# S5 output matrix made on GpSimd, with its power chain and the S5 steps set later, in a two-block transformer kernel

## Chip, cores and metric

One core of a Trainium2 chip runs the whole program. The metric is the device time of one execution in microseconds; the kernel before takes 1207.07 us (median of 3 runs, 1204.92 to 1209.34).

## What is computed

The input is 256 tokens of width 1024. A first block mixes two branches, an S5 layer (a diagonal complex state-space scan over 32 groups of 64 states) and an mLSTM, then does cross attention and a convolutional feed-forward; two more layers follow. The change touches only the S5 branch of the first block:

```python
a_bar = jnp.exp(lam * dt)
b_bar = ((a_bar - 1.0) / lam)[..., None] * b_mat
bu = jnp.einsum('blgh,gph->blgp', ug, b_bar)
_, states = lax.associative_scan(combine, (a_seq, bu), axis=1)
y = jnp.einsum('blgp,ghp->blgh', states, c_mat).real + d * ug
```

and, beside it, the projection `proj = h @ w_in` from which the S5 input, the mLSTM's queries, keys, values and gates and the branch gates come.

## The kernel before

All matrix products are done in split float32: each weight tile is loaded to `raw` on SP's queue, ScalarE rounds it to a high half `hi` (L321), VectorE takes the low half `lo` = raw - hi (L322), and TensorE runs three matmuls per 128-row step (L329 to L331 feature-major, L338 to L340 token-major). So every weight tile of 128x1024 costs ScalarE, VectorE and TensorE one turn each. PSUM has three tiles of tag `g` for projections and four of tag `a` for small work.

The first block's projections come in this order: two pairs of tiles for the S5 input U (L1679 evacuates); four pairs for queries and keys, each evacuated by `ev_qk`: a product into `msg` (L1689), ScalarE's first tap (L1695), six taps on VectorE (L1697), ScalarE's tanh back into `msg` (L1699) and a last product (L1700). `msg` has one buffer, so the next pair's L1689 waits until the pair before is through L1700. Then the token-major columns: `w_vif` (values and mLSTM gates, 264 wide), `w_tm` 1, 2 and 3 (values, two halves of the output gate). Then come the S5 scan, the mLSTM, eight pairs of gate projections, and the S5 output.

The S5 steps lie between. `s5_prep` makes on VectorE the powers `pz` of the transition and the input factors `cz`, and on GpSimd the chain of squarings `ak`, `ax` (L719 to L723) that the scan multiplies with. `s5_inputs(b)`, for b = 0 and 1, forms from `pz`, `cz` and the constants four outer products on VectorE, each of two products and one sum or difference (L754, L755): the output matrices CR and CN, 128x640 elements each, and the input matrices, two of 128x512. ScalarE copies each into block-diagonal tiles (L764 into CR, L767 into CN, L772 into `w4`), half of the partitions at a time. TensorE then transposes (L779) and forms the short-range kernel (L785, L787), and ScalarE copies these out (L780, L790). `s5_state` passes U through DRAM into U2 by five DMAs issued on ScalarE's queue and multiplies it (L805) into the states ST. `s5_scan` combines ST in ten steps on VectorE (L815 to L818), and `s5_output` reads CR, CN, KS and ST (L842) after the gate projections.

The order of work on each engine is not written by hand. A planner gives every instruction the priority of its place in the program (raised for weight loads), goes through the program with its own estimate of durations, and puts on each engine the instruction of highest priority among those that are ready; the order is then fixed, and each engine works through its list, waiting where it must. A tile with a tag and one buffer can be given out again only when all readers of the tile before it in that tag are done. So ST, `so` (two buffers), `hs` (one) and `msg` (one) set waits as well as the data does.

Of the kernel before, what the change touches and what calls it, by code (L numbers as in the profile page):

```python
# [20 lines left out]
P = 128  # L21
# [236 lines left out]
def _program(ctx, tc, nc, a, offs, dump):  # L258
# [21 lines left out]
    mult, add, sub = ALU.mult, ALU.add, ALU.subtract  # L280
# [359 lines left out]
    def s5_prep(bp):  # L640
# [42 lines left out]
        G.memset(pz[:, 0, :, 0:1], 1.0)  # L683
        G.memset(pz[:, 1, :, 0:1], 0.0)

        def cmul(o, x_, y_, conj=False, tt=tt):
            sh = list(o.shape)
            n_ = len(sh) > 3 and sh[3] or 1
            u, v = [T(bp, sh, "cm%d_%d" % (n_, q_), bufs=2 if n_ == 1 else 1) for q_ in range(2)]
            tt(u, x_, y_, op=mult)  # L690
            tt(v, x_, y_[:, ::-1], op=mult)
            if conj:
                tt(o[:, 0], u[:, 0], u[:, 1], op=add)
                tt(o[:, 1], v[:, 1], v[:, 0], op=sub)
            else:
                tt(o[:, 0], u[:, 0], u[:, 1], op=sub)
                tt(o[:, 1], v[:, 0], v[:, 1], op=add)
# [15 lines left out]
        cmul(cz[:, :, :, 2], cz[:, :, :, 3], p1)  # L713
        cmul(cz[:, :, :, 0:2], cz[:, :, :, 2:4], sq2)
        cmul(pz[:, :, :, 3:5], pz[:, :, :, 1:3], sq2)
        NL = 5
        ak = T(bp, [P, NL, 2, 16], "ak")
        ax = T(bp, [P, NL, 2, 16], "ax")
        G.tensor_copy(ak[:, 0], pz[:, :, :, 4])  # L719
        for k in range(1, NL):  # L720
            cmul(ak[:, k], ak[:, k - 1], ak[:, k - 1], tt=G.tensor_tensor)
        G.tensor_copy(ax[:, :, 0], ak[:, :, 1])
        G.tensor_scalar(ax[:, :, 1], ak[:, :, 1], -1.0, None, op0=mult)  # L723
        return pz, cz, ak, ax

    def s5_zero(bp):
        CR = T(bp, [P, 16, 5, 2, 16], "CR")
        CN = T(bp, [P, 16, 5, 2, 16], "CN")
        KS = T(bp, [P, 16, P], "KS")
        bt = [T(bp, [P, 2, 4, 4, 2, 16], "w4%d" % q) for q in range(2)]  # L730
        ST = T(bp, [P, 2, 16, 65], "ST")
        V.memset(ST[:, :, :, 0:1], 0.0)
        V.memset(CR, 0.0)
        G.memset(KS, 0.0)
        G.memset(CN, 0.0)
        for q in range(2):
            V.memset(bt[q], 0.0)
        return CR, CN, KS, bt, ST

    def s5_steps(bp, K5, U, prep, zero):  # L740
        pz, cz, ak, ax = prep
        CR, CN, KS, bt, ST = zero
        NL = 5
        VR = T(bp, [P, 16, P], "gs")
        VI = T(bp, [P, 16, P], "gm")
# [4 lines left out]
        def outer(xa, ya, xb, yb, nt, op):  # L750
# [4 lines left out]
            tt(m[0], m[0], m[1], op=op)  # L755
            return m[0]

        def inputs(b):
            s8 = slice(8 * b, 8 * b + 8)
            cr, ci, br, bi = cz[:, 0, s8], cz[:, 1, s8], b_re[:, s8, :], b_im[:, s8, :]  # L760
            pr, pi, xr, xi = pz[:, 0, s8], pz[:, 1, s8], c_re[:, s8, :], c_im[:, s8, :]
            m = outer(pr, xr, pi, xi, 5, sub)
            for g, hs in halves:
                ACT.copy(CR[hs, s8, :, g, :], m[hs])  # L764
            m = outer(pr, xi, pi, xr, 5, add)
            for g, hs in halves:
                ACT.copy(CN[hs, s8, :, g, :], m[hs])  # L767
            for r_, ops in enumerate(((cr, br, ci, bi, 4, sub), (cr, bi, ci, br, 4, add))):
# [24 lines left out]

        def state():
            us = T(dr, [16, 32, 4, 64], "us")
            U2 = box["U2"] = T(bp, [P, 16, 64], "U2")
            nc.scalar.dma_start(us.rearrange("(a j) q t c -> (j q) a (t c)", a=4),
                                U.rearrange("p a t c -> p a (t c)"))
            for t in range(4):
                nc.scalar.dma_start(U2[32 * t:32 * t + 32], us.rearrange("a q t c -> t q a c")[t])  # L800
            for b in range(4):
                vp = T(pa, [P, 2, 4, 64], "a")
                for r_, W in enumerate((VR, VI)):
                    for q in range(4):
                        mm(vp[:, r_, q, :], W[:, 4 * b + q, :], U2[:, 4 * b + q, :], start=True, stop=True)  # L805
                ACT.copy(ST[:, :, 4 * b:4 * b + 4, 1:], vp)

        def combine(k, d0, n_):
            d = 1 << k
            dst = ST[:, :, :, d0:d0 + 2 * d * (n_ - 1) + 1:2 * d]  # L810
            src = ST[:, :, :, d0 - d:d0 - d + 2 * d * (n_ - 1) + 1:2 * d]
            sh = [P, 2, 16, n_]
            t1 = T(bp, [P, 2, 16, 32], "w40")[:, :, :, :n_]
            t2 = T(bp, [P, 2, 16, 32], "w41")[:, :, :, :n_]
            tt(t1, src, bc(ak[:, k, 0][:, None, :, None], sh), op=mult)  # L815
            tt(t2, src[:, ::-1], bc(ax[:, k][:, :, :, None], sh), op=mult)
            tt(dst, dst, t1, op=add)
            tt(dst, dst, t2, op=add)  # L818
# [7 lines left out]
                    combine(k, 3 << k, n_)  # L826

        def output():
            U2 = box["U2"]
            y = T(bp, [P, 4, S], "w40")  # L830
            Y4 = T(bp, [P, 4, 4, 64], "w41")
            for b in range(2):
# [819 lines left out]
    with ExitStack() as ph:  # L1652
# [48 lines left out]

        for j in range(4):
            gemm_pairs("w_fm", [2 + j], 8, xh, xl, lambda _, ps, j=j: ev_qk(j, ps))
            if j >= 2:
                s5_inputs(j - 2)
        vm = T(bp, [P, 2, 4, 132], "vm")
        G.memset(vm[:, :, :, 128:132], 1.0)
        og = T(bp, [P, 2, 512], "og")
# [21 lines left out]
                ts(o, o, 0.5, 0.5, op0=mult, op1=add)  # L1730

        gemm_tm("w_vif", range(1), xh, xl, ev_vif, cw=264)
        s5_state()
        gemm_tm("w_tm", range(1, 2), xh, xl, ev_vm)
        gemm_tm("w_tm", range(2, 4), xh, xl, ev_o)
        s5_scan()
        ymh, yml = mlstm(bp, b2, K5, ifs, qk, vm, og)
        gs = T(bp, [P, 8, S], "gs")
# [110 lines left out]
```

## Time and profile before

| what | value |
|---|---|
| median of 3 runs | 1207.07 us (1204.92 to 1209.34) |
| the profiled execution's own time | 1207.08 us |
| its span, first to last instruction | 1205.3 us |
| TensorE (PE) busy | 1165.0 us, 97% |
| VectorE (DVE) busy | 888.5 us, 74% |
| ScalarE (ACT) busy | 692.3 us, 57% |
| GpSimd (POOL) busy | 73.1 us, 6% |
| mean granted TensorE clock | 0.991 |

The profile calls the engines PE (TensorE's matmuls), PEld (its weight loads), DVE (VectorE), ACT (ScalarE), POOL (GpSimd) and SP (the queue that loads weights). Times are microseconds from the start of the span. In a time line a row gives start, duration, engine, line, operation, written tile <- read tiles with the shape; a bracket at its end gives how long the engine had been idle and whom it waited for. A tile's buffer number is left out, and names may be cut at a digit (`w` for `w40`, `cs` for `cs5`).

### The profile page before, as it was taken

The page shows a single profiled execution, that of the slowest core. Times are in us where ns is not written, and L with a number is a line of the kernel's source. Part 1 is how long each engine was busy: PE and PEld are TensorE (multiplying, and loading weights), DVE is VectorE, ACT ScalarE, POOL GpSimd, SP SyncE. Part 2 cuts the span into 40 slices and gives each one's busy share as a digit, 9 for nine tenths or more (in the row PEclk, how much of TensorE's full clock was granted, in tenths as well). Part 3 has the DMA queues.
Part 4 walks back from the last instruction along what each step waited for, and adds up shares of the span by engine and source line. Part 5 has one row for each costly group of instructions (what it writes and reads, how often), then busy time and mean ns, then how long its engine had stood idle before and what let it go on. Part 6 is the DMA issues. An engine that isn't in the chain of part 4 may idle for free.

```text
span 1205.3 us, 23538 instructions
## 1 busy us (share of the span) xinstructions
PE 1165.0 (97%) x9370; PEld 1106.2 (92%) x9370; DVE 888.5 (74%) x1685; ACT 692.3 (57%) x1229; POOL 73.1 (6%) x80
## 2 busy tenths in 40 slices
PE   7899999999999999999999899999999999999997
PEld 7889989999999998899988899998988789999986
DVE  8979857866688887667565886666697868976654
ACT  5684645655565765446355675554686666755441
POOL 4400000100000000000001000001000001000010
PEclk9999999999999999999999999999999999999998
DMA  7524435654356556656433466666863225666561
GB/s 269 156 73 154 159 117 186 215 184 140 122 166 203 180 184 174 196 180 213 163 92 108 160 186 182 179 182 190 296 202 107 67 74 184 203 191 178 161 204 36
DMA packets 61276, 199.41 MB, mean 165 GB/s; under 512 B 8502, under 2 KB 12398, under 8 KB 60910
## 3 DMA queue, kind: packets, MB, share of 16 engines
q1 hardware_dynamic: 54864, 191.60, 50.1%
q10 hardware_dynamic: 6302, 6.32, 1.6%
q8 instruction: 73, 1.20, 0.4%
q14 instruction: 37, 0.30, 0.1%
HBM read 196.28 MB, written 1.60 MB: 164 GB/s over the span
## 4 chain that ended last, share of the span: by engine, by line
PE 87%; DVE 6%; ACT 3%; issue 2%; DMA 1%; POOL 1%; DVEq 0%; SPq 0%; ACTq 0%
PE g L330 12%; PE g L329 12%; PE g L331 12%; PE a L329 7%; PE a L330 7%; PE a L331 7%; PE a L394 5%; PE g L394 4%; PE a L396 3%; PE g L340 2%; PE g L338 2%; PE g L339 2%; DVE lo L322 2%; PE g L396 2%; PE m L1150 1%
## 5 line engine op out<-in xcount | busy, mean ns | idle before, releaser
L322 DVE TENSOR_TENSOR lo<-raw,hi 128x1024 fp32r<-128x1024 f32 (+3 forms) x359 | 428.4, 1199 | 181.9 <-ACT hi L321 179.5
L321 ACT CAST hi<-raw 128x1024 fp32r<-128x1024 f32 (+3 forms) x359 | 363.6, 1020 | 341.5 <-PE g L330 127.7
L329 PE MATMUL g<-xh,hi 128*128 128x256 f32 (+1 forms) x616 | 176.0, 286 | 8.3 <-ACT xh L569 8.0
L330 PE MATMUL g<-xl,hi 128*128 128x256 f32 (+1 forms) x624 | 178.3, 286 | 0.3
L331 PE MATMUL g<-xh,lo 128*128 128x256 f32 (+1 forms) x616 | 175.3, 285 | 1.4 <-DVE lo L322 1.4
L329 PE MATMUL a<-nh,hi 128*128 128x256 f32 x560 | 159.4, 285 | 4.7 <-ACT sqa L1075 2.8
L330 PE MATMUL a<-nl,hi 128*128 128x256 f32 x560 | 158.8, 284 | 0.9 <-DVE nl L517 0.9
L331 PE MATMUL a<-nh,lo 128*128 128x256 f32 x560 | 158.7, 284 | 0.0
L329 PEld LDWEIGHTS g<-xh,hi 128*128 128x128 f32 x616 | 117.2, 190 | 9.6 <-ACT xh L569 8.0
L330 PEld LDWEIGHTS g<-xl,hi 128*128 128x128 f32 x624 | 118.9, 190 | 1.6 <-DVE xl L570 0.8
L331 PEld LDWEIGHTS g<-xh,lo 128*128 128x128 f32 x616 | 116.9, 190 | 2.4 <-DVE lo L322 2.0
L329 PEld LDWEIGHTS a<-nh,hi 128*128 128x128 f32 x560 | 108.1, 193 | 5.7 <-ACT sqa L1075 2.9
L330 PEld LDWEIGHTS a<-nl,hi 128*128 128x128 f32 x560 | 108.1, 193 | 1.1 <-DVE nl L517 1.1
L331 PEld LDWEIGHTS a<-nh,lo 128*128 128x128 f32 x560 | 108.0, 193 | 0.0
L394 PE MATMUL a<-mx,hi 128*128 128x512 f32 x264 | 91.9, 394 | 0.0
L329 PE MATMUL g<-nh,hi 128*128 128x256 f32 x288 | 81.5, 283 | 0.0
L330 PE MATMUL g<-nl,hi 128*128 128x256 f32 x288 | 81.5, 283 | 0.0
L331 PE MATMUL g<-nh,lo 128*128 128x256 f32 x288 | 81.5, 283 | 0.0
L396 PE MATMUL a<-mx,lo 128*128 128x256 f32 x264 | 73.1, 277 | 0.0
L394 PE MATMUL g<-mx,hi 128*128 128x512 f32 x198 | 69.0, 395 | 0.0
L394 PEld LDWEIGHTS a<-mx,hi 128*128 128x128 f32 x264 | 49.4, 188 | 11.5
L329 PEld LDWEIGHTS g<-nh,hi 128*128 128x128 f32 x288 | 55.3, 192 | 0.0
(619 smaller groups left out, 2863.8 us busy)
## 6 DMA issues: line engine op xcount, KB each, us to landing
raw<-g_up SPq DMA_DIRECT2D x88, 512.0 KB, 3.6
raw<-f_up SPq DMA_DIRECT2D x44, 512.0 KB, 3.5
raw<-g_dn SPq DMA_DIRECT2D x32, 512.0 KB, 3.6
raw<-w_fm SPq DMA_DIRECT2D x27, 512.0 KB, 3.7
raw<-ev_fm SPq DMA_DIRECT2D x20, 512.0 KB, 3.7
raw<-f_dn SPq DMA_DIRECT2D x16, 512.0 KB, 3.5
raw<-od_fm SPq DMA_DIRECT2D x14, 512.0 KB, 4.4
raw<-g_dn SPq DMA_DIRECT2D x16, 384.0 KB, 3.3
```

What stands on the lines that cost most here:

```text
L321: ACT.copy(hi, raw)
L322: tt(lo, raw, hi, op=sub)
L329: mm(ps, hi[:, o:o + P], xh[:, k, :], start=start and k == 0, stop=False, skip_group_check=skip)
L330: mm(ps, hi[:, o:o + P], xl[:, k, :], start=False, stop=False, skip_group_check=skip)
L331: mm(ps, lo[:, o:o + P], xh[:, k, :], start=False, stop=stop and k == kt - 1, skip_group_check=skip)
L338: mm(ps, xh[:, k, t], hi[:, wsl], start=start and j == 0, stop=False, skip_group_check=skip)
L339: mm(ps, xh[:, k, t], lo[:, wsl], start=False, stop=False, skip_group_check=skip)
L340: mm(ps, xl[:, k, t], hi[:, wsl], start=False, stop=stop and j == len(ks) - 1, skip_group_check=skip)
L394: mm(f2, hi[:, o], X[:, k].rearrange("p a s -> p (a s)"), start=first and j == 0, stop=False, skip_group_check=True)
L396: mm(ps[:, 0, :], lo[:, o], X[:, k, 0, :], start=False, stop=last and j == len(ks) - 1, skip_group_check=True)
L1150: mm(o[64 * r:64 * r + 64, :], v0, pT[:, 0:S], start=first, stop=False, skip_group_check=True)
```

## The change

CR is taken out of the S5 input step. Right after the tiles of the S5 steps are set up, GpSimd forms for each of the two blocks the two products (128x640) and two differences, the latter for 64 partitions each and written straight into CR's diagonal blocks; VectorE's three operations and ScalarE's two copies for it, per block, are gone. The squarings `ak`, `ax` come after that on GpSimd, in a function of their own, with scratch of their own (`uv`). The scratch `sp`, then `uv`, then ST share one tag with one buffer, so ST is made, and its first column cleared, in the state step. The first input step comes after all four query/key pairs, the second after `w_tm` 1, the state step after `w_tm` 2, and `w_tm` 3 after it.

```diff
--- before.py
+++ after.py
@@ -683,10 +683,10 @@
         G.memset(pz[:, 0, :, 0:1], 1.0)
         G.memset(pz[:, 1, :, 0:1], 0.0)
 
-        def cmul(o, x_, y_, conj=False, tt=tt):
+        def cmul(o, x_, y_, conj=False, tt=tt, uv=None):
             sh = list(o.shape)
             n_ = len(sh) > 3 and sh[3] or 1
-            u, v = [T(bp, sh, "cm%d_%d" % (n_, q_), bufs=2 if n_ == 1 else 1) for q_ in range(2)]
+            u, v = uv or [T(bp, sh, "cm%d_%d" % (n_, q_), bufs=2 if n_ == 1 else 1) for q_ in range(2)]
             tt(u, x_, y_, op=mult)
             tt(v, x_, y_[:, ::-1], op=mult)
             if conj:
@@ -713,33 +713,36 @@
         cmul(cz[:, :, :, 2], cz[:, :, :, 3], p1)
         cmul(cz[:, :, :, 0:2], cz[:, :, :, 2:4], sq2)
         cmul(pz[:, :, :, 3:5], pz[:, :, :, 1:3], sq2)
+        return pz, cz, cmul
+
+    def s5_powers(bp, pz, cmul):
         NL = 5
         ak = T(bp, [P, NL, 2, 16], "ak")
         ax = T(bp, [P, NL, 2, 16], "ax")
-        G.tensor_copy(ak[:, 0], pz[:, :, :, 4])
+        uv = T(bp, [P, 3, 2, 16], "ST")
+        G.tensor_copy(uv[:, 2], pz[:, :, :, 4])
+        G.tensor_copy(ak[:, 0], uv[:, 2])
         for k in range(1, NL):
-            cmul(ak[:, k], ak[:, k - 1], ak[:, k - 1], tt=G.tensor_tensor)
+            cmul(ak[:, k], ak[:, k - 1], ak[:, k - 1], tt=G.tensor_tensor, uv=(uv[:, 0], uv[:, 1]))
         G.tensor_copy(ax[:, :, 0], ak[:, :, 1])
         G.tensor_scalar(ax[:, :, 1], ak[:, :, 1], -1.0, None, op0=mult)
-        return pz, cz, ak, ax
+        return ak, ax
 
     def s5_zero(bp):
         CR = T(bp, [P, 16, 5, 2, 16], "CR")
         CN = T(bp, [P, 16, 5, 2, 16], "CN")
         KS = T(bp, [P, 16, P], "KS")
         bt = [T(bp, [P, 2, 4, 4, 2, 16], "w4%d" % q) for q in range(2)]
-        ST = T(bp, [P, 2, 16, 65], "ST")
-        V.memset(ST[:, :, :, 0:1], 0.0)
         V.memset(CR, 0.0)
         G.memset(KS, 0.0)
         G.memset(CN, 0.0)
         for q in range(2):
             V.memset(bt[q], 0.0)
-        return CR, CN, KS, bt, ST
+        return CR, CN, KS, bt
 
     def s5_steps(bp, K5, U, prep, zero):
-        pz, cz, ak, ax = prep
-        CR, CN, KS, bt, ST = zero
+        pz, cz, cmul = prep
+        CR, CN, KS, bt = zero
         NL = 5
         VR = T(bp, [P, 16, P], "gs")
         VI = T(bp, [P, 16, P], "gm")
@@ -755,14 +758,22 @@
             tt(m[0], m[0], m[1], op=op)
             return m[0]
 
+        sp = T(bp, [P, 2, 8, 5, 16], "ST")
+        for b in range(2):
+            s8 = slice(8 * b, 8 * b + 8)
+            pr, pi, xr, xi = pz[:, 0, s8], pz[:, 1, s8], c_re[:, s8, :], c_im[:, s8, :]
+            sh = [P, 8, 5, 16]
+            m = sp[:, 0], sp[:, 1]
+            for t, x_, y_ in ((m[0], pr, xr), (m[1], pi, xi)):
+                G.tensor_tensor(t, bc(x_[:, :, :, None], sh), bc(y_[:, :, None, :], sh), op=mult)
+            for g, hs in halves:
+                G.tensor_tensor(CR[hs, s8, :, g, :], m[0][hs], m[1][hs], op=sub)
+        ak, ax = s5_powers(bp, pz, cmul)
+
         def inputs(b):
             s8 = slice(8 * b, 8 * b + 8)
             cr, ci, br, bi = cz[:, 0, s8], cz[:, 1, s8], b_re[:, s8, :], b_im[:, s8, :]
-            pr, pi, xr, xi = pz[:, 0, s8], pz[:, 1, s8], c_re[:, s8, :], c_im[:, s8, :]
-            m = outer(pr, xr, pi, xi, 5, sub)
-            for g, hs in halves:
-                ACT.copy(CR[hs, s8, :, g, :], m[hs])
-            m = outer(pr, xi, pi, xr, 5, add)
+            m = outer(pz[:, 0, s8], c_im[:, s8, :], pz[:, 1, s8], c_re[:, s8, :], 5, add)
             for g, hs in halves:
                 ACT.copy(CN[hs, s8, :, g, :], m[hs])
             for r_, ops in enumerate(((cr, br, ci, bi, 4, sub), (cr, bi, ci, br, 4, add))):
@@ -793,6 +804,8 @@
 
         def state():
             us = T(dr, [16, 32, 4, 64], "us")
+            ST = box["ST"] = T(bp, [P, 2, 16, 65], "ST")
+            V.memset(ST[:, :, :, 0:1], 0.0)
             U2 = box["U2"] = T(bp, [P, 16, 64], "U2")
             nc.scalar.dma_start(us.rearrange("(a j) q t c -> (j q) a (t c)", a=4),
                                 U.rearrange("p a t c -> p a (t c)"))
@@ -806,6 +819,7 @@
                 ACT.copy(ST[:, :, 4 * b:4 * b + 4, 1:], vp)
 
         def combine(k, d0, n_):
+            ST = box["ST"]
             d = 1 << k
             dst = ST[:, :, :, d0:d0 + 2 * d * (n_ - 1) + 1:2 * d]
             src = ST[:, :, :, d0 - d:d0 - d + 2 * d * (n_ - 1) + 1:2 * d]
@@ -826,7 +840,7 @@
                     combine(k, 3 << k, n_)
 
         def output():
-            U2 = box["U2"]
+            U2, ST = box["U2"], box["ST"]
             y = T(bp, [P, 4, S], "w40")
             Y4 = T(bp, [P, 4, 4, 64], "w41")
             for b in range(2):
@@ -1701,8 +1715,7 @@
 
         for j in range(4):
             gemm_pairs("w_fm", [2 + j], 8, xh, xl, lambda _, ps, j=j: ev_qk(j, ps))
-            if j >= 2:
-                s5_inputs(j - 2)
+        s5_inputs(0)
         vm = T(bp, [P, 2, 4, 132], "vm")
         G.memset(vm[:, :, :, 128:132], 1.0)
         og = T(bp, [P, 2, 512], "og")
@@ -1730,9 +1743,11 @@
                 ts(o, o, 0.5, 0.5, op0=mult, op1=add)
 
         gemm_tm("w_vif", range(1), xh, xl, ev_vif, cw=264)
+        gemm_tm("w_tm", range(1, 2), xh, xl, ev_vm)
+        s5_inputs(1)
+        gemm_tm("w_tm", range(2, 3), xh, xl, ev_o)
         s5_state()
-        gemm_tm("w_tm", range(1, 2), xh, xl, ev_vm)
-        gemm_tm("w_tm", range(2, 4), xh, xl, ev_o)
+        gemm_tm("w_tm", range(3, 4), xh, xl, lambda _, ps: ev_o(1, ps))
         s5_scan()
         ymh, yml = mlstm(bp, b2, K5, ifs, qk, vm, og)
         gs = T(bp, [P, 8, S], "gs")
```

## Rows read from the trace of the kernel before

**Rows 1.** Windows: busy time of each engine, granted clock, DMA share, GB/s, by stretch.
```profile
30.00:47.20 17.20, 17.01 (x144) 16.79 (x144) 17.20 (x24) 11.67 (x17) 12.84 (x19) 1.00 0.63 180
47.20:62.60 15.40, 10.32 (x73) 9.20 (x71) 14.62 (x26) 11.63 (x24) 0.00 (x0) 0.89 0.32 105
51.00:54.00 3.00, 2.58 (x12) 2.61 (x13) 2.97 (x6) 2.93 (x7) 0.00 (x0) 0.50 0.67 261
62.60:71.40 8.80, 7.66 (x57) 6.52 (x57) 3.80 (x8) 8.62 (x17) 0.00 (x0) 1.00 0.00 0
84.00:130.00 46.00, 46.00 (x371) 44.23 (x371) 45.75 (x86) 21.10 (x38) 1.64 (x1) 1.00 0.38 125
```

**Rows 2.** Waits of PE from 40 to 100 us: total, times, longest.
```profile
PE g L338 <- DVE msg L1689: 3.7, 1, 3.7
PE a L779 <- ACT w L772: 1.3, 1, 1.3
PE g L339 <- DVE lo L322: 1.1, 1, 1.1
```

**Rows 3.** Time line of DVE, 50 to 63 us.
```profile
50.59 0.68 DVE L1689 TENSOR_TENSOR msg<-g,rs 128x512 f32<-128x512 f32 x1
51.19 0.81 DVE L754 TENSOR_TENSOR hs<-pz,cs 128x640 f32<-128x640 f32 x1
...
62.58 0.69 DVE L1689 TENSOR_TENSOR msg<-g,rs 128x512 f32<-128x512 f32 x1
```

**Rows 4.** Lines of DVE, 29.6 to 62.6 us: count | busy us, mean ns | idle.
```profile
L754 DVE TENSOR_TENSOR so<-pz,cs 128x640 f32<-128x640 f32 x4 | 3.3, 832 | 0.0
L754 DVE TENSOR_TENSOR hs<-pz,cs 128x640 f32<-128x640 f32 x4 | 3.3, 832 | 0.0
```

**Rows 5.** Lines of ACT, 29.6 to 84 us.
```profile
L764 ACT COPY CR<-so 64x640 f32<-64x640 f32 x4 | 2.9, 719 | 0.0
```

**Rows 6.** Time line of POOL, 0 to 150 us.
```profile
9.48 1.28 POOL L474 TENSOR_TENSOR sqa<-sq,sq 128x512 f32<-128x512 f32 x1 [1.42 <-ACT sq L488]
...
29.81 0.76 POOL L719 COPY ak<-pz 128x32 f32<-128x32 f32 x1 [10.66 <-DVE pz L697]
...
33.27 0.22 POOL L697 TENSOR_TENSOR ak<-cm 128x16 f32<-128x16 f32 x1
...
42.37 0.85 POOL L723 TENSOR_SCALAR ax<-ak 128x80 f32<-128x80 f32 x1
74.87 1.67 POOL L307 TENSOR_TENSOR mz<-ebase,na 128x8 f32<-128x8 f32 x1 [31.66 <-DVE na L873]
```

**Rows 7.** Time line of POOL, two of the later 128x512 sums.
```profile
211.28 2.04 POOL L474 TENSOR_TENSOR sqa<-sq,sq 128x512 f32<-128x512 f32 x1 [65.07 <-ACT sq L488]
...
324.19 2.17 POOL L474 TENSOR_TENSOR sqa<-sq,sq 128x512 f32<-128x512 f32 x1 [53.09 <-ACT sq L488]
```

**Rows 8.** Time line of DVE beside POOL's work.
```profile
34.49 1.27 DVE L322 TENSOR_TENSOR lo<-raw,hi 128x1024 fp32r<-128x1024 f32 x1
...
210.10 2.07 DVE L570 SCALAR_TENSOR_TENSOR ol<-mem,consts,oh 128x256 fp32r<-128x256 f32 x5
...
325.12 1.53 DVE L534 SCALAR_TENSOR_TENSOR xl<-x,consts,xh 128x256 fp32r<-128x256 f32 x1
```

**Rows 9.** Source lines L322 and L534, whole run: ns min/median/max.
```profile
L322 DVE TENSOR_TENSOR lo<-raw,hi x359: 671/1225/2321, 5.9 to 1181.0; 128x1024 fp32r<-128x1024 f32 x158, 128x768 fp32r<-128x768 f32 x18, 128x512 fp32r<-128x512 f32 x1, 128x792 fp32r<-128x792 f32 x1
...
L534 DVE SCALAR_TENSOR_TENSOR xl<-x,consts,xh x32: 467/478/1532, 321.5 to 1005.8; 128x256 fp32r<-128x256 f32 x32
```

**Rows 10.** Time lines of PE and DVE and chain: first readers, the scan's ends.
```profile
55.64 0.41 PE L785 MATMUL a<-CR,w 128*32 128x128 f32 x2
...
84.33 1.23 DVE L815 TENSOR_TENSOR w<-ST,ak 128x1024 f32<-128x1024 f32 x1
...
128.47 1.19 DVE L818 TENSOR_TENSOR ST<-ST,w 128x992 f32<-128x992 f32 x1
...
155.67 0.56 PE a L842 x26
```

## The prediction

> **What bounds the kernel now.** I read the windows first, then TensorE's waits, then the time lines of VectorE, GpSimd and ScalarE in the stretch that the change touches. From 84 to 130 us TensorE is busy all the time [rows 1], and so it is, nearly, to the end of the run: time can only be won or lost where TensorE stands still before that. The reader should compare the five stretches of [rows 1]: from 30 to 47.2 TensorE and VectorE are both full (17.0 and 17.2 of 17.2 us); from 47.2 to 62.6 TensorE falls to 10.3 of 15.4 us while VectorE is still at 14.6; from 62.6 to 71.4 it is ScalarE that is full (8.6 of 8.8) and VectorE has room (3.8). The waits name the gaps [rows 2]: 3.7 us for the evacuation `msg` (L1689), 1.3 us for ScalarE's copy into the block matrices (L772), 1.1 us for a low half (L322), together 6.1 us. The longest has a second price: from 51 to 54 the granted clock was 0.50, that is 1.2 GHz, after TensorE had stood still, and 12 matmuls took 2.58 us there [rows 1]. At 2.4 GHz one takes 46.00 / 371 = 0.124 us, so 2.58 - 12 x 0.124 = 1.1 us went there. Everything that this change can win here is therefore at most 6.1 + 1.1 = 7.2 us.
>
> Why `msg` is late: its buffer is single, so the four query/key pairs are evacuated one chain after the other, the second at 50.59 and the third at 62.58 us [rows 3]. By 47 TensorE has all three PSUM tiles of `g` filled and must wait for the second. Between these evacuations VectorE does the 24 S5 operations (L754, L755) as they come ready. So VectorE's work from 30 to 62 us is the price that counts.
>
> **What is taken from VectorE.** The CR half of the inputs is, for each of two blocks, two products and one difference of 128x640. From [rows 4]: four products x 0.832 and two differences, which I take at the same price, being of the same size: 5.0 us. Neighbours overlap by 0.08 us (50.59 + 0.68 against the next start 51.19, [rows 3]), so six give 5.0 - 0.5 = 4.5 us of the engine's time. ScalarE loses four copies of 0.719 us [rows 5]. Two belong to the second block, just ahead of the stretch where ScalarE is full: 1.4 us that count; the other two lie where ScalarE has room (11.7 of 17.2 us, [rows 1]) and count nothing.
>
> **What GpSimd gets.** Four products of 128x640 and four differences of 64x640. The nearest row is a sum of 128x512: 1.28 us with the engine free; a 16-element operation takes 0.22 [rows 6]. That is (1.28 - 0.22) / 496 = 2.1 ns an element, and 1.55 us for 640. The broadcast operands and the strided output have no row here; I take them at the same rate. For the halves I take the full 1.55 too, since 640 elements lie along each partition; the lower bound is that two halves, on different partitions, run beside each other, as two instead of four. The engine itself is free for it: the work can start where the power chain starts now, at 29.81 [rows 6].
>
> **What that does to VectorE** is the term that decides. GpSimd's 128x512 sums in this trace lengthen a VectorE operation that reads two SBUF operands. At 324.19 one ran 2.17 us instead of 1.28, because it waited for the L322 in progress; then L534 on VectorE took 1.53 us where its median is 0.48 [rows 7 to 9]: 1.05 us lost. Of 13 such sums 11 lengthened a VectorE operation, by 0.5 to 1.1 us. Scaled by 2.1 ns x 128 elements, a 640 sum costs 1.05 + 0.27 = 1.32 us. VectorE is full from 30 to 62, and nearly all that it does there (L322, L754, L755, L1697) reads two SBUF operands, so each GpSimd operation meets one. Eight x 1.32 = 10.6 us; with overlapping halves six x 1.32 = 7.9; if GpSimd always waited for gaps, 0. Nothing in a shared resource could make VectorE faster than alone, so 0 is the lower end. I take 10.6: the 11 cases are far more than the two, and no row shows two GpSimd operations side by side.
>
> The Trainium skill (SBUF — State Buffer, Who interferes with whom) has the two engines share a port as an exclusive lock for a whole instruction, and its GPSIMD Engine Reference (Performance versus the Vector engine) gives about 2.6 cycles an element at 1.2 GHz. An estimate from these pages is 1.39 us per operation, 11.1 us for eight, and a total 0.5 us later than mine. The trace agrees on the lock for large operands, but not for "a whole instruction": the power chain's small operations, back to back from 29.81 to 43.2, left L322 at 1.27 us against its median of 1.23 [rows 6, 8, 9].
>
> **The power chain** (now 29.81 to 43.2, [rows 6]) starts when CR is done: eight operations of 1.55 us, each after one VectorE operation of some 0.9 us (between 0.7 for `msg` and 1.23 for L322, [rows 3, 9]), is 20 us, so at about 50; it ends near 63 with the same durations and one more copy (0.76). Its first reader, the scan, starts at 84.33 [rows 10]; cover 21 us, no cost. CR of the first block is needed at 55.64 [rows 10] and is made by about 40: no cost. The memset of ST's first column now needs the chain's end, because `uv` and `sp` take ST's place; it goes to VectorE's queue somewhere in the state step. Its cost is 0 if it is queued after 63, and a stall of everything behind it on VectorE if before (rival below). The state step with its 64 matmuls, and its five DMA issues on ScalarE's queue, goes behind two more token projections. Each is 48 matmuls x 0.124 = 6 us, so 12 us; the scan would end near 142 to 146 instead of 129.7, and the output reads it at 155.67 [rows 10]: covered by some 10 us. No DMA on SP's or GpSimd's queue is moved; GpSimd's next work is at 74.87 [rows 6], after the chain. The setting of the two input steps behind the projections changes whom TensorE and ScalarE prefer when two things are ready, and I know of no row that prices that, so I give it 0 and bound it by the 1.3 + 1.1 us of gaps that it could close.
>
> **The sum.** -4.5 (VectorE) + 10.6 (port) - 1.4 (ScalarE) = +4.7 us at the point where the third `msg` frees TensorE (62.58 now). TensorE has work for nearly all the time after it, so what is lost there stays lost. The profiled execution took 1207.08 us with a span of 1205.3; the median of the runs is 1207.07, so the sum stands on either: **1211.7 us**.
>
> **Rivals.** (a) *The port is not the price, VectorE's relief is.* VectorE with a queue of ready operations goes first and GpSimd waits. For it speaks the sum at 211.28: five L570 in a row took 2.07 us, 0.41 each, and GpSimd took 2.04 [rows 7, 8]. Against it speak 11 of 13. The Trainium skill (SBUF — State Buffer, Who interferes with whom) says that issue order, not shape, decides who blocks; both rows bear it out. Then -4.5, and the gap of 3.7 falls so far that the clock stays up, -1.1: -5.6, 1201.5 us. This decides if the port takes under about 1 us from VectorE in all; at 4.5 the two cancel. (b) *No change that can be measured.* The port costs 7.9 (halves beside each other), or the later input steps close the gaps of 1.3 and 1.1 us: +4.7 - 2.6 or - 2.4, about +2.2, 1209.3 us. (c) *A new wait.* The ST memset reaches VectorE's queue before the power chain is done. Then everything behind it waits, L322 and so TensorE too, until the 20 small operations are through: 20 x 0.22 to 0.3 us with VectorE quiet, some 5 us on top: 1216.7. (d) CR comes too late for its matmuls: only if GpSimd took three times as long; folded into (c).
>
> **How the numbers follow.** About 0.3% (3.6 us) is what a measurement here can tell from no change. Chances: forecast 0.38, (c) and (d) 0.06, (b) 0.28, (a) 0.28. So faster 0.28, same 0.28, slower 0.44. The forecast's own range is 1209 to 1214 (six to eight port waits, with or without the 1.4). The range over all cases reaches down to (a), with a little of its 7.2 us ceiling, and up to (c): 1200.8 to 1217.
>
> **What would show it.** In the new profile VectorE operations beside GpSimd's 640-element ones should read about 2.0 us where they were 0.7 to 1.2, eight times between 30 and 50; the second `msg` should come near 57 to 61 instead of 50.6, and TensorE's waits before 72 should sum to 9 to 12 us, part of them now for L322. If instead GpSimd's operations take 2.5 us or more each while VectorE's keep their lengths, and the second `msg` comes before 50, (a) holds and I am wrong at the port term. A VectorE wait for a GpSimd operation ahead of the ST memset would show (c).

## The result: 0.5% slower, and the profile after

The changed kernel takes 1214.72 us (median of 14 runs, 1212.69 to 1217.74), the kernel before, in the same sessions, 1208.19 us (1204.92 to 1212.70). The ratio is 1.0054 with a 95% interval of 1.0045 to 1.0062, so +5.4 to +7.5 us. The forecast, +4.7 us against a profiled execution of 1207.08, was 1211.7; the profiled execution after is 1212.69, with a span of 1210.9 against 1205.3. The measured median lies within the range over all cases (1200.8 to 1217) and 0.7 us above the forecast's own range (1209 to 1214); between the medians the kernel lost 6.5 us where 4.7 were forecast. The sign and the mechanism were right; the terms were not all of the right size, and the runs below set them.

The windows of the kernel after, over two of the stretches of [rows 1], show where it goes (columns as there: PE, PEld, DVE, ACT, POOL, then granted clock, DMA share, GB/s):

```profile
30.00:47.20 17.20, 10.84 (x74) 10.42 (x73) 17.20 (x13) 6.51 (x8) 16.64 (x12) 0.88 0.37 107
47.20:62.60 15.40, 15.40 (x119) 14.67 (x119) 14.83 (x25) 11.05 (x23) 10.70 (x18) 0.91 0.52 166
```

From 30 to 47.2 TensorE falls from 17.0 to 10.8 us, and its clock to 0.88. VectorE is full as before, but gets 13 instructions done there instead of 24. GpSimd, at 16.6, is full beside it. In the next window TensorE makes up for a part (15.4 instead of 10.3 us). The new places of the S5 steps are not the reason: e2 below, with the steps at their old places, has the same 15.4:

```profile
47.20:62.60 15.40, 15.40 (x128) 14.55 (x128) 14.84 (x25) 11.32 (x23) 10.59 (x17) 1.00 0.51 168
```

TensorE's waits from 20 to 206 us, after:

```profile
PE g L331 <- DVE lo L322: 7.4, 4, 3.2
PE g L338 <- DVE ifs L1729: 1.7, 1, 1.7
PE a L856 <- issue: 1.7, 1, 1.7
PE a L790 <- ACT w L783: 1.0, 1, 1.0
```

The wait for `msg` and the one on L339 of [rows 2] are gone. Two waits for a low half, 3.2 and 3.1 us, stand in their place, ahead of the matmuls at 38.71 and 46.78. Behind each the granted clock was 0.50, that is 1.2 GHz (windows 40 to 43 and 47 to 49); the kernel before had one such stretch there, from 51 to 54 [rows 1]. VectorE's time line says why they are late:

```profile
30.48 1.91 DVE L757 TENSOR_TENSOR so<-pz,cs 128x640 f32<-128x640 f32 x1
32.31 1.90 DVE L757 TENSOR_TENSOR hs<-pz,cs 128x640 f32<-128x640 f32 x1
34.13 2.04 DVE L757 TENSOR_TENSOR so<-cz,cs 128x512 f32<-128x512 f32 x1
36.10 0.68 DVE L1703 TENSOR_TENSOR msg<-g,rs 128x512 f32<-128x512 f32 x1
36.70 1.95 DVE L322 TENSOR_TENSOR lo<-raw,hi 128x1024 fp32r<-128x1024 f32 x1
38.58 1.90 DVE L758 TENSOR_TENSOR so<-so,hs 128x640 f32<-128x640 f32 x1
40.40 3.20 DVE L1711 SCALAR_TENSOR_TENSOR mcv<-msg,consts,mcv 128x255 f32<-128x255 f32 x2
43.53 2.02 DVE L757 TENSOR_TENSOR hs<-cz,cs 128x512 f32<-128x512 f32 x1
45.47 1.25 DVE L322 TENSOR_TENSOR lo<-raw,hi 128x1024 fp32r<-128x1024 f32 x1
...
56.87 0.09 DVE L808 MEMSET ST<- 128x32 f32 x1 [0.57 <-POOL ak L697]
...
57.84 0.68 DVE L1703 TENSOR_TENSOR msg<-g,rs 128x512 f32<-128x512 f32 x1
...
68.58 0.68 DVE L1703 TENSOR_TENSOR msg<-g,rs 128x512 f32<-128x512 f32 x1
```

and GpSimd's over the same time:

```profile
29.43 4.10 POOL L768 TENSOR_TENSOR ST<-pz,cs 128x640 f32<-128x640 f32 x2 [10.60 <-issue]
33.61 3.97 POOL L770 TENSOR_TENSOR CR<-ST 64x640 f32<-64x640 f32 x2
37.66 3.95 POOL L768 TENSOR_TENSOR ST<-pz,cs 128x640 f32<-128x640 f32 x2
41.69 3.31 POOL L770 TENSOR_TENSOR CR<-ST 64x640 f32<-64x640 f32 x2
45.06 0.57 POOL L723 COPY ST<-pz 128x32 f32<-128x32 f32 x1
```

While GpSimd works on CR, from 29.4 to 45.0, the VectorE operations with two operands in SBUF that start from 30.48 on take 1.9 to 2.0 us, but for the two taps of L1711, which take 3.20 together, where a product of 128x640 took 0.83 [rows 4], one of 128x512 takes 0.68 (e6, below), and L322 took 1.23 [rows 9]. The one operation that reads PSUM, `msg` at 36.10, keeps its 0.68. Once GpSimd goes on to the small operations of the power chain, L322 is back at 1.25. Against their lengths before, the eight lengthened operations lose 1.08 + 1.07 + 1.35 + 0.73 + 1.08 + 2.33 (two taps of L1711, 0.86 together in f1) + 1.33 = 9.0 us, 1.12 each.

The third `msg` comes at 68.58 instead of 62.58 [rows 3], 6.0 us late. To follow a change to the end of the first block I use a later mark: SP issues the transfer of `mem`, with which cross attention begins. Before:

```profile
201.13 0.33 SPq L966 DMA_DIRECT2D mem<-mem  x1
```

and after:

```profile
205.14 0.33 SPq L980 DMA_DIRECT2D mem<-mem  x1
```

So the first block costs 4.0 us more. The windows from 20 us to this mark, before, then after:

```profile
20.00:201.13 181.13, 171.13 (x1674) 163.17 (x1673) 147.47 (x282) 102.95 (x184) 17.97 (x22) 0.98 0.44 140
20.00:205.14 185.14, 172.57 (x1670) 164.07 (x1669) 150.60 (x274) 99.84 (x180) 34.23 (x31) 0.98 0.43 136
```

TensorE stands still for 10.0 us before (181.13 less 171.13 busy) and for 12.6 after (185.14 less 172.57). The remaining 1.4 is busy time; the granted clock is 0.98 in both windows, so the clock does not explain it, and its cause stays open. The rest of the span adds 5.6 - 4.0 = 1.6 us, to which I come back.

### The profile page after: what moved, and what is told of

Same layout as the page of the kernel before. It is cut to its first block, busy times and chain, and to the rows that moved or that the text cites. A ratio compares the mean times of both kernels' runs of the same rounds, so it can differ in the third digit from the quotient of the medians.

```text
span 1210.9 us, 23541 instructions
## 1 busy us (share of the span) xinstructions
PE 1169.1 (97%) x9370; PEld 1109.6 (92%) x9370; DVE 892.0 (74%) x1679; ACT 688.3 (57%) x1225; POOL 88.3 (7%) x89
## 4 chain that ended last, share of the span: by engine, by line
PE 84%; DVE 8%; ACT 3%; issue 2%; DMA 1%; POOL 1%; DVEq 0%; SPq 0%; ACTq 0%
PE g L330 11%; PE g L331 11%; PE g L329 11%; PE a L329 7%; PE a L330 7%; PE a L331 7%; PE a L394 5%; PE g L394 4%; DVE lo L322 3%; PE a L396 3%; PE g L338 2%; PE g L340 2%; PE g L339 2%; PE g L396 2%; PE m L1164 1%
## 5 line engine op out<-in xcount | busy, mean ns | idle before, releaser
L322 DVE TENSOR_TENSOR lo<-raw,hi 128x1024 fp32r<-128x1024 f32 (+3 forms) x359 | 429.0, 1200 | 182.2 <-ACT hi L321 174.5
```

Source lines behind the costliest of these rows:

```text
L322: tt(lo, raw, hi, op=sub)
```

## The experiments

The theory: GpSimd's large operations hold up VectorE's, and the price of the change is eight such delays, less what VectorE and ScalarE are relieved of. The rivals: the new places of the S5 steps are the price; or GpSimd is merely late with CR; or any GpSimd work there would do the same, whatever it reads. A second group asks whether the work, moved out of the full stretch altogether, would win anything. The table has the `mem` mark of each profile against 201.13, and the ratio to the kernel before with its interval.

| kernel | `mem` mark, us | ratio | 95% interval |
|---|---|---|---|
| after | 205.14, +4.0 | 1.0054 | 1.0045 to 1.0062 |
| e1_cr_on_dve | 202.19, +1.1 | 1.0073 | 1.0055 to 1.0091 |
| e2_order_before | 204.55, +3.4 | 1.0054 | 1.0042 to 1.0066 |
| e3_no_cr | 197.16, -4.0 | 0.9990 | 0.9974 to 1.0006 |
| e4_products_only | 201.25, +0.1 | 1.0014 | 1.0003 to 1.0025 |
| e5_memsets | 205.51, +4.4 | 1.0042 | 1.0027 to 1.0057 |
| e6_memsets_after_pz | 197.40, -3.7 | 0.9980 | 0.9971 to 0.9990 |
| f1_late_cr_dve | 202.26, +1.1 | 1.0011 | 0.9998 to 1.0025 |
| f2_late_cr_pool | 210.54, +9.4 | 1.0148 | 1.0123 to 1.0173 |
| f3_late_ks | 203.07, +1.9 | 1.0094 | 1.0077 to 1.0111 |
| f4_late_cr_scan_last | 202.15, +1.0 | 1.0023 | 1.0015 to 1.0032 |
| f5_scan_last | 199.90, -1.2 | 1.0007 | 0.9997 to 1.0017 |
| f6_after_scan_last | 206.21, +5.1 | 1.0066 | 1.0053 to 1.0080 |

Each mark comes from one execution. How far they can be trusted is seen from kernels that differ only in the place of the scan: the third `msg` comes at 62.58 and 62.71 (before, f5) and at 68.58 and 68.51 (after, f6), but the `mem` marks differ by 1.2 and 1.1 us. So I take differences of about 1 us at the mark for no more than scatter, unless the third `msg` or the ratios say the same.

### CR back on VectorE, the steps where the change puts them

In the kernel after:

```diff
-        for b in range(2):
-            ...
-            for g, hs in halves:
-                G.tensor_tensor(CR[hs, s8, :, g, :], m[0][hs], m[1][hs], op=sub)
...
+            m = outer(pz[:, 0, s8], c_re[:, s8, :], pz[:, 1, s8], c_im[:, s8, :], 5, sub)
+            for g, hs in halves:
+                ACT.copy(CR[hs, s8, :, g, :], m[hs])
```

> Order of the steps, the shared ST tag and the late power chain as in the changed kernel, CR formed on VectorE and copied by ScalarE as before. Theory 1 (the shared port is the price, the order costs nothing): the eight long GpSimd operations are gone, VectorE has its 4.5 us back to do, so close to the kernel before, 1206 to 1210 us. Theory 2 (the later setting of the steps is the price): stays at 1213 to 1216 us.

In the first block it went as the port theory has it: +1.1 instead of +4.0, the third `msg` at 63.20. The whole, 1216.23 us or 1.0073, did not: it is no faster than the kernel after, as the second theory would have it. The loss comes behind the mark. From `mem` to the first load of `x_wk` it is 15.2 us here, 6.2 before. ScalarE's line there:

```profile
209.68 3.30 ACT L569 ACTIVATE oh<-mem,consts 128x256 fp32r<-128x256 f32 x8 [5.53 <-DMA mem<-mem]
```

and TensorE's wait from 200 to 225:

```profile
PE g L329 <- ACT hi L321: 6.6, 1, 6.6
```

The planner has set the splits of `mem` (L569) ahead of the next weight's high half on ScalarE. They wait for a transfer, and TensorE waits behind them. Nothing was edited there; as far as the trace shows, another order 130 us earlier tipped the planner. e1, f2 and f3 have this order; so I read the first block by its mark, and the whole only between kernels that agree behind it. Of the 13.4 us that e1's profile loses behind the mark against the one before, 9.0 are this; the other 4.4 were not followed, and its profiled execution, 1221.64 us, lies 5.4 above the median of e1.

### CR on GpSimd, the steps where they were before

```diff
+            if j >= 2:
+                s5_inputs(j - 2)
-        s5_inputs(0)
...
         gemm_tm("w_vif", range(1), xh, xl, ev_vif, cw=264)
+        s5_state()
         gemm_tm("w_tm", range(1, 2), xh, xl, ev_vm)
-        s5_inputs(1)
...
```

> CR on GpSimd with the power chain behind it, but the S5 steps placed in the program as before. Theory 1 (port): as slow as the changed kernel, 1212 to 1217 us, VectorE's operations beside GpSimd's again about 1.9 us long. Theory 2 (order): back to 1207 to 1210 us.

The ratio is that of the kernel after, 1.0054, and the mark is 0.6 us earlier. Second and third `msg` are at 57.74 and 68.47. So the later places are worth about nothing with CR on GpSimd; with it on VectorE, e1 says, they cost 0.6 us at the third `msg` and 1.1 at the mark. As rival for the 4.0 us they fall.

### No CR at all; the products alone

e3 replaces all eight GpSimd operations by one tiny memset for each block, so CR stays zero and that part of the S5 output is left out. e4 keeps the four products and leaves out the four differences, with the same part of the output missing:

```diff
             for t, x_, y_ in ((m[0], pr, xr), (m[1], pi, xi)):
                 G.tensor_tensor(t, bc(x_[:, :, :, None], sh), bc(y_[:, :, None, :], sh), op=mult)
-            for g, hs in halves:
-                G.tensor_tensor(CR[hs, s8, :, g, :], m[0][hs], m[1][hs], op=sub)
```

> The changed kernel with none of the eight CR operations on GpSimd (the output matrix CR stays zero, so that part of the S5 output is left out); all else stays. Theory 1 (port): only the relief is left, VectorE 4.5 us and ScalarE 1.4 us, so below the kernel before: 1201 to 1205 us, no TensorE wait for L322 over 1 us between 20 and 60 us. Theory 2 (order, or the new ST wait): 1212 us or more.

> The changed kernel with the four products on GpSimd but without the four differences (CR stays zero, that part of the S5 output is left out). Theory 1 (port, each operation costs VectorE about 1.1 us): half of the way from the kernel without CR to the changed one, about 1207 to 1210 us. Rival 1b (only the differences hurt, by their strided writes): as fast as without CR. Rival 1c (the two halves of a difference run beside each other and cost like one): two thirds of the way.

The marks are 197.16, 201.25 and 205.14 for none, four and eight operations: 4.1 us for the four products, 3.9 for the four differences. That is 1.0 us of end of block each. At the third `msg` (61.02, 63.95, 68.58) the same steps are 2.9 and 4.6 us, and the ratios of the three kernels put 2.9 and 4.8 us on them. So all eight cost 7.6 to 8.0 us by any of the three; how they divide is not settled, but the differences, on 64 partitions, cost about as much as the products or more. e3 itself missed what was expected: its median of 1206.05 is 1.0 above the range, TensorE still waits 1.8 us for one L322, and with its interval of 0.9974 to 1.0006 the relief alone is no sure gain. GpSimd's products in e4 took 1.90 us each beside VectorE:

```profile
29.62 7.60 POOL L768 TENSOR_TENSOR ST<-pz,cs 128x640 f32<-128x640 f32 x4 [10.64 <-issue]
```

With e1 the change falls into three steps, by marks that follow one another: the new places of the S5 steps 201.13 to 202.19, +1.1; CR off VectorE and ScalarE 202.19 to 197.16, -5.0; the eight operations on GpSimd 197.16 to 205.14, +8.0.

### GpSimd busy for as long, but only writing

Here eight memsets of 128x2080 stand for the eight operations (CR zero again). In the first version (e5) nothing made them wait:

```diff
-        sp = T(bp, [P, 2, 8, 5, 16], "ST")
+        sp = T(bp, [P, 2080], "ST")
...
-            ...
+            for _ in range(4):
+                G.memset(sp, 0.0)
```

> The changed kernel with the eight CR operations on GpSimd replaced by eight memsets of 128x2080 on the scratch (about 1.8 us each by the 128x2048 memset of the kernel before; CR stays zero, that part of the S5 output is left out). GpSimd is then busy for about as long at the same place, but reads nothing. Theory 1 (VectorE waits for GpSimd's reads of operands): as the kernel without CR, 1204 to 1208 us, VectorE's operations at their usual 0.7 to 1.2 us beside the memsets. Rival (any busy GpSimd operation on large tiles holds VectorE up, writes too): 1212 to 1216 us.

It failed as an experiment: with no input, the memsets ran as soon as GpSimd was free, from 4.99 to 29.6 us, so they hit the making of `pz` instead. The last four of them on GpSimd:

```profile
22.07 7.53 POOL L767 MEMSET ST<- 128x2080 f32 x4
```

VectorE beside them:

```profile
22.59 1.22 DVE L322 TENSOR_TENSOR lo<-raw,hi 128x1024 fp32r<-128x1024 f32 x1 [0.25 <-issue]
...
28.05 1.57 DVE L708 TENSOR_SCALAR a<-pz 128x16 f32<-128x16 f32 x1
```

The 16-element operation with one input (L708), 0.17 us in the kernel after, took 1.57 beside a memset. The Trainium skill (SBUF — State Buffer, Who interferes with whom) lists copies and tensor_scalar among the operations that can take the shared ports for themselves and then contend with any GpSimd access; this row agrees. `pz` was done at 36.3 us instead of 29.4. That has a second reason: GpSimd's own earlier operations stood behind memsets, and `s5er` (L307), from which `pz` is made, was done at 19.7 instead of 16.8. How the +4.4 divides between the two was not tried, and e5 does not decide the question.

In the second version (e6) a small copy from `pz` into the same tile stands ahead, so the memsets run where CR ran:

```diff
         sp = T(bp, [P, 2080], "ST")
+        G.tensor_copy(sp[:, 0:32].rearrange("p (a j) -> p a j", a=2), pz[:, :, :, 4])
```

> As the kernel with eight memsets instead of the CR operations, but the scratch is first written from pz, so that the memsets cannot be set before pz is made and stand where the CR operations stood (CR stays zero, that part of the S5 output is left out). Theory 1 (it is GpSimd's reading of operands that VectorE's two-operand operations wait for): VectorE's L322, L757, L758 keep 0.7 to 1.25 us beside the memsets; second msg at 48 to 52 us, memory transfer of the next stage within 2 us of the kernel without CR (197.2 us). Rival (any busy GpSimd): operations of 1.9 us, second msg at 56 us or later, transfer at 204 us or later.

GpSimd is now as busy as with CR:

```profile
30.43 15.14 POOL L768 MEMSET ST<- 128x2080 f32 x8
```

and VectorE beside it is as fast as without:

```profile
30.98 0.81 DVE L757 TENSOR_TENSOR hs<-pz,cs 128x640 f32<-128x640 f32 x1
31.71 0.68 DVE L757 TENSOR_TENSOR so<-cz,cs 128x512 f32<-128x512 f32 x1
...
32.91 1.21 DVE L322 TENSOR_TENSOR lo<-raw,hi 128x1024 fp32r<-128x1024 f32 x1
34.05 0.81 DVE L758 TENSOR_TENSOR so<-so,hs 128x640 f32<-128x640 f32 x1
```

The mark is at 197.40, that of e3 with no GpSimd work at all. So neither GpSimd's time nor its writes are the price, and what is left is its reads. (A memset does no arithmetic either, and a GpSimd operation that reads a single operand was not tried.) The ratios agree: after, 1.0054, is 8.9 us behind e6, 0.9980. e6 also settles the lateness of the power chain, which here starts behind 15 us of memsets and delays nothing. By the same section of the Trainium skill a VectorE operation with two SBUF inputs contends with a GpSimd operation that reads SBUF and not with one that only writes it; e6 agrees.

### CR formed after the mLSTM has been queued

f1 starts from the kernel before. CR (VectorE and ScalarE) and KS, which needs it, are formed behind the mLSTM in the program; the four input columns that KS needs are kept by eight small GpSimd copies. f2 is f1 with CR on GpSimd, straight into the halves. f3 moves only KS.

```diff
+        B3 = [T(tp, [P, 2, S], "sqa", bufs=2)... for _ in range(2)]
...
-            m = outer(pr, xr, pi, xi, 5, sub)
-            for g, hs in halves:
-                ACT.copy(CR[hs, s8, :, g, :], m[hs])
...
-                kp = T(pa, [32, 4, P], "a")
-                ...
+                for r_ in range(2):
+                    G.tensor_copy(B3[r_][:, s4], bt[q4][:, r_, :, 3].rearrange("p q g h -> p q (g h)"))
...
         ymh, yml = mlstm(bp, b2, K5, ifs, qk, vm, og)
+        s5_late_cr(tt)
+        s5_late_ks()
```

> The kernel before with CR, and the short-range kernel KS that reads it, formed after the mLSTM in the program instead of in the input steps; CR stays on VectorE and ScalarE (8 small GpSimd copies keep the input columns that KS needs). Theory 1 (what counts is VectorE's queue from 30 to 62 us): the 4.5 us leave that stretch and no port is taken, so the first block ends 4 to 6 us earlier than before: 1201 to 1205 us. Rival (VectorE and ScalarE are as short later): 1207 us or more.

> As the kernel before it in this list, but the late CR on GpSimd (the same eight operations as in the changed kernel). Theory 1 (the port costs VectorE about 1 us for each operation wherever both run, but only counts where VectorE is what others wait for): VectorE operations beside it lengthened, the total close to the late CR on VectorE, 1202 to 1208 us. Rival (eight long GpSimd operations cost 8 us wherever they stand): 1209 to 1213 us.

> As the late CR on VectorE, but CR stays in the input steps on VectorE; only KS is formed late, which takes its 16 copies off ScalarE between 57 and 78 us. Theory 1: VectorE's 24 operations stay in the way of the second and third evacuation, so about as before, 1204 to 1208 us. Rival (ScalarE's full stretch is what counts): 1200 to 1204 us.

f1 won nothing. The second and third `msg` are 2.3 and 3.3 us earlier (48.26, 59.32), but then TensorE waits:

```profile
PE a L971 <- DVE hn L970: 5.7, 2, 5.5
```

VectorE's outputs of the mLSTM, `hn`, start hardly earlier in f1 than before, the first at 146.2 against 146.9. f1, then before, by the view of the tile (name of the group, ns min/median/max, first and last start):

```profile
L970 DVE TENSOR_SCALAR hn<-hs,mlsr x8: 276/286/290, 146.2 to 151.2; 128x128 f32<-128x128 f32 x8
```

```profile
L951 DVE TENSOR_SCALAR hn<-hs,mlsr x8: 281/286/287, 146.9 to 154.7; 128x128 f32<-128x128 f32 x8
```

From 84 to 130 VectorE is busy 45.05 of 46 us in f1 as it was before (45.75, [rows 1]): behind the projections the scan and the mLSTM fill it, and what starts earlier ends no earlier. The wait of 5.7 us is most of the 7.2 that the gaps were worth.

f2 against f1 has the eight operations on GpSimd at another place, and CR's work off VectorE and ScalarE; the mark is 210.54 - 202.26 = 8.3 us later. Its GpSimd line:

```profile
57.84 1.27 POOL L766 TENSOR_TENSOR so<-pz,cs 128x640 f32<-128x640 f32 x1
...
61.65 1.45 POOL L766 TENSOR_TENSOR so<-pz,cs 128x640 f32<-128x640 f32 x1
63.17 3.31 POOL L773 TENSOR_TENSOR CR<-so,so 64x640 f32<-64x640 f32 x2
66.56 3.54 POOL L766 TENSOR_TENSOR so<-pz,cs 128x640 f32<-128x640 f32 x2
...
74.36 3.52 POOL L773 TENSOR_TENSOR CR<-so,so 64x640 f32<-64x640 f32 x2
```

and VectorE there:

```profile
58.00 1.67 DVE L1719 SCALAR_TENSOR_TENSOR x<-msg,mcv 128x512 f32<-128x512 f32 x1 [0.28 <-ACT msg L1718]
...
61.44 5.32 DVE L1716 SCALAR_TENSOR_TENSOR mcv<-msg,consts,mcv 128x255 f32<-128x255 f32 x4
66.69 2.29 DVE L322 TENSOR_TENSOR lo<-raw,hi 128x1024 fp32r<-128x1024 f32 x1
68.90 1.88 DVE L1716 SCALAR_TENSOR_TENSOR mcv<-msg,consts,mcv 128x253 f32<-128x253 f32 x2
...
74.25 4.30 DVE L1716 SCALAR_TENSOR_TENSOR mcv<-msg,consts,mcv 128x255 f32<-128x255 f32 x4 [0.67 <-ACT mcv L1714]
```

The product at 57.84 found VectorE idle and went through in 1.27 us; the operation that VectorE began at 58.00 took 1.67, where the same one takes 0.68 in f1. Four taps take 5.32 beside the product and the differences from 61.65 on (two take 0.86 in f1), and the L322 at 66.69 takes 2.29 instead of 1.22. With the taps at 68.90 and 74.25 VectorE is lengthened by 0.99 + 3.60 + 1.07 + 1.02 + 2.58 = 9.3 us in all, 1.16 for each of GpSimd's eight. The 8.3 us at the mark are not the price of these alone: VectorE and ScalarE have less to do than in f1, and TensorE waits 4.5 us between 80 and 120 for high halves on ScalarE, which f1 does not have:

```profile
PE g L338 <- ACT hi L321: 4.5, 2, 4.0
```

Of what f2 loses behind the mark, 6.8 us are the order on ScalarE that e1 has. f3 missed too: +1.9 at the mark, and 9 us behind it by the same order.

### The scan behind the mLSTM

f4, f5 and f6 are f1, before and after with one line moved:

```diff
-        s5_scan()
         ymh, yml = mlstm(bp, b2, K5, ifs, qk, vm, og)
+        s5_scan()
```

> The late CR on VectorE, and in addition the S5 scan set behind the mLSTM in the program. Theory (the late CR won 13 us up to the last gate projections and lost them because the mLSTM's chain on VectorE ends no earlier than before, TensorE waiting 5.7 us for hn): with the scan out of its way hn comes earlier, the wait falls below 2 us, the next stage's memory transfer is issued at 194 to 198 us and the whole takes 1201 to 1206 us. Rival (VectorE is simply full to 150 us, whatever the order): the scan is late instead, TensorE waits for the output, and nothing is won: 1208 to 1212 us.

> The kernel before with nothing but the scan set behind the mLSTM. Theory (in the kernel before TensorE does not wait for either, it is full from 84 to 155 us): the same, 1205 to 1211 us; a gain above 3 us would say that the order of scan and mLSTM matters by itself.

> The changed kernel with the scan set behind the mLSTM. Theory 1 (its loss is all made before 70 us, at the port): no help, 1212 to 1217 us. Rival (the later state step is part of the loss, through the scan): 1208 to 1211 us.

If the scan were what holds up `hn` in f1, f4 should have freed it. It did not: TensorE's wait for `hn` is 5.7 us as in f1, and `hn` starts at 146.5, where its last wait is for `mlsr` from GpSimd, as it is in f1:

```profile
146.46 0.48 DVE L970 TENSOR_SCALAR hn<-hs,mlsr 128x128 f32<-128x128 f32 x2 [2.52 <-POOL mlsr L506]
```

So it is not the scan's place. From 130 to 146 VectorE is busy only 9.9 of 16 us in f1, so a full VectorE is not the whole reason either. That leaves the mLSTM's own chain over several engines; which of its steps sets the time was not tried. f5 is the kernel before in time, f6 the kernel after. Of the kernels that compute all of the output none beats the kernel before.

## Why the prediction was right, and where its terms were off

**VectorE is what bounds the stretch.** Right. It was full from 30 to 47.2 before and after, and TensorE's idle time follows it.

**The port term, +10.6: the mechanism is shown, the size was too large.** e3 to after is 8.0 us at the mark, 7.6 at the third `msg` and 7.7 by the ratios, that is 1.0 an operation where I took 1.32. Two steps are in this. The lengthening on VectorE is 1.12 each (9.0 in all), not 1.05 scaled up to 1.32; the scaling supposed that VectorE waits out a whole GpSimd operation at 2.1 ns an element, and a product that meets nothing is 1.27 us (f2), not the 1.55 that I worked out: 640 elements with broadcast operands take the time of the 512-element sum in [rows 6]. And 9.0 us of VectorE came to 8.0 at the end of the block, a difference that the marks do not resolve. The observed length, 1.9 to 2.0 us for six of the eight between 30 and 46 and 1.6 on average for the other two, is about what was forecast.

The prediction also read the power chain as a case against a lock held for a whole instruction, since L322 took 1.27 us beside it instead of 1.23. The rows do not carry that. An operation of 16 elements on GpSimd took 0.22 us at 33.27 [rows 6], and another of the same shape, before:

```profile
34.64 1.20 POOL L696 TENSOR_TENSOR ak<-cm 128x16 f32<-128x16 f32 x1
```

So there it was GpSimd that waited, and at 2.1 ns an element, the prediction's own rate, 16 elements could hold VectorE up by some 0.03 us (an estimate).

**The halves.** I took each half at the full price against a lower bound in which two run beside each other. Right: beside a busy VectorE a pair of halves took 3.97, 3.31 and, in f2, 3.31 and 3.52 us, and two full products 4.10, 3.95 and, in f2, 3.54; and four differences cost about as much as four products or more (e3, e4, after).

**The relief, -4.5 - 1.4: too large, by 0.9 at the mark and by 3.7 where it was forecast.** e1 to e3 is -5.0 us at the mark. At the third `msg` the same step is 63.20 to 61.02, -2.2 only (e6, with the same relief, has 59.60, so this split is uncertain by 1.4). So the sum at the third `msg`, +4.7, was right in part by errors that cancel: measured there, +0.6 for the places (62.58 to 63.20), -2.2 for the relief, +7.6 for GpSimd (61.02 to 68.58), in all +6.0. At the end of the block it is +1.1 - 5.0 + 8.0 = +4.0 (the unrounded marks). What I said of time lost there staying lost fails by these 2 us. A part is given back from L842 on, where the kernel before ran at a lower clock. Before:

```profile
155.00:176.00 21.00, 18.84 (x474) 17.82 (x473) 9.69 (x14) 8.52 (x12) 0.00 (x0) 0.92 0.28 89
```

and after:

```profile
155.00:180.00 25.00, 22.88 (x516) 21.50 (x515) 13.38 (x23) 11.70 (x16) 0.00 (x0) 1.00 0.32 105
```

At 0.92 instead of 1.00, 18.84 us of matmuls hold 18.84 x 0.08 = 1.5 us that the kernel after does not pay there.

**The places of the steps, 0 with a bound of -2.4.** With CR on VectorE (e1) +0.6 at the third `msg` and +1.1 at the mark; with it on GpSimd (e2 against after) +0.1 and +0.6. The bound covered a gain alone, and none came; a small loss is all that these marks allow.

**The power chain, the CR deadline and the scan.** Right, and early: CR was done at 45.0 (forecast about 50), the chain ran from 45.06 to 58.2 (50 to 63), the scan's last sum ended at 144.0 (142 to 146). None delayed TensorE by a wait of its own; the chain held up VectorE once, for 0.6 us (next).

**The rivals.** (a) needed the port to cost under about 1 us in all; it cost 8, and the VectorE rows beside GpSimd, 1.9 to 2.0 us, say the same. (b) needed the halves to overlap, or the places to win; neither shows. (c) happened in small: VectorE waited 0.6 us ahead of ST's memset for the end of the chain, not 5, since the memset's turn came at 56.87, with the chain nearly done.

**The waits.** Forecast 9 to 12 us before 72, partly for L322: measured 6.4 + 1.7 + 1.0 = 9.1, of which 6.4 for L322. The second `msg` came at 57.84 (57 to 61).

**Behind the first block** I forecast nothing, and 1.6 us more came in the profiles. Nothing ties it to the change. Where the order on ScalarE is the old one, the other profiles differ there from the one before by -0.2 (e5) to +5.4 us (f5, in which only the scan was moved), and the profiled execution before, 1207.08, lies 1.1 below its median. A part shows at a wait that both kernels have, where the clock came back later: after is 4.03 us behind at the L322 ahead of it (684.17, 688.20) and 4.79 at one behind it (713.74, 718.53). Before:

```profile
684.00:690.00 6.00, 4.71 (x26) 4.34 (x25) 6.00 (x15) 3.10 (x6) 0.00 (x0) 0.72 0.39 133
```

and after, the window 4.05 us later:

```profile
688.05:694.05 6.00, 4.97 (x23) 4.44 (x23) 6.00 (x15) 3.07 (x6) 0.00 (x0) 0.51 0.40 128
```

The rest stays open.

## What to carry to other kernels

Before work goes from a full VectorE to an idle GpSimd, ask what it reads. Two-operand work from SBUF takes its time back from VectorE's own two-operand operations: here, at the end of the first block, the relief of VectorE and ScalarE was worth 5.0 us and GpSimd's operations cost 8.0. Work that only writes costs VectorE's two-operand operations nothing, but a small one-input operation beside it can pay (e5). And where an order is planned by a program, judge an edit by marks close behind it as well as by the total, for an unrelated turn later can cost more than the edit.

## What was not expected of the hardware

- GpSimd's writes alone left VectorE's two-operand operations at 0.81 and 1.21 us (e6), yet made a 128x16 operation with one input take 1.57 us instead of 0.17 (e5).
- Operations on the two halves of the partitions follow one another on GpSimd, and half the partitions save little beside a busy VectorE: 3.31 to 3.97 us for two halves, 3.54 to 4.10 for two products of 128 partitions (after, f2). No run shows a half that meets nothing; a full product that met nothing took 1.27 (f2).
- After the same wait of 2.8 us, ahead of the same work, the clock was granted at 0.72 in one kernel and 0.51 in the other over the same 6 us.
